# Moving part of the differential attention's weights and of its sub-norm from VectorE to ScalarE and GpSimd

## The chip, the cores and the metric

The kernel runs on one core of a Trainium2 chip. The metric is the device time of one execution in microseconds (us). The engines are called as in the profile: PE (TensorE, matrix products; PEld is its weight load), DVE (VectorE), ACT (ScalarE), POOL (GpSimd) and SP (SyncE, which issues most DMAs). Each engine works through its own queue in order.

## The reference

One layer of a diffusion backbone: 512 latent tokens and 256 context tokens, width 2048, float32. A modulated RMSNorm feeds two mixers: differential attention (8 heads) and latent attention (8 heads); both go through one output projection into the residual stream, and a gated MLP with a short convolution follows. What matters here, cut:

```python
def _diff_attend(q, k, v, lam):
    ...
    w = jax.nn.softmax(s1, axis=-1) - lam * jax.nn.softmax(s2, axis=-1)
    return jnp.einsum('bhqk,bhkd->bhqd', w.astype(v.dtype), v)
...
def _merge_heads(o_da, o_mla, subln_w, lambda_init):
    o_da = _rmsnorm(o_da, subln_w) * (1.0 - lambda_init)
    ...
    return jnp.concatenate([o_da, o_mla], axis=-1)
```

So each differential head makes two softmax maps, subtracts the second times lambda from the first, and multiplies by the values; each head's output is then normed over its 128 features (the sub-norm) and scaled.

## The kernel before, in words

Nearly every product is computed in three passes, from a rounded high part and a rest of each operand (`split`, L77; `mm3`, L101). ACT rounds (L80, L83), DVE subtracts (L81, L84). The layer runs in stages: norm and modulation, input projection, differential attention, latent attention, output projection, MLP. In the stages touched by the change the program is written head by head, and the framework's scheduler decides the order of the instructions on each engine; in the first stage and from the end of the output projection on, the order on PE, ACT, DVE and SP is written out by hand.

**Differential attention** (`da_head`, L551). A head has 4 blocks of 128 queries. For each block `scores_softmax` (L506) is called twice, once per map: four matmuls into a PSUM tile `s` of two buffers (L510), the negated row maximum on DVE (L512), the exponential on ACT with its row sum (L514). DVE takes the reciprocal of both sums (L566). POOL scales the second map by its reciprocal and by minus lambda (L567). Then L568, the changed line, scales the first map and adds the second in one DVE instruction, in place. The tile of the first map, `p0`, has 8 buffers (two heads), that of the second 3. When the four blocks are there, `weighted_values` (L517) goes over the 6 blocks of 128 keys: four transposes on PE into `pt`, which has one buffer (L522), rounding on ACT (L80, `wth`), rest on DVE (L81, `wtl`), and three matmuls with the values into `po` (L104 to L106). ACT copies the output (L525) and SP stores it to DRAM (`o_d`, L572). Between these, PE works on the query projection of the coming heads (`feature`, L457; the matmuls `f<-a2k`); after the last head's projection there is no more of this work.

**Latent attention** (L657 to L674) has the same shape with one map per head. DVE normalises the map (L667, L668). Per pair of heads `latent_pair` (L591) makes queries, keys and values. Between the maps and the weighted values of each head stands `sub_norm(h)` (L646) for the differential head of the same number: load `o_d`, square on ACT (L651), sum over the partitions with a matmul against ones (L653), then `rstd` (L157) and the application (L655).

`rstd` computes the inverse root by a logarithm and an exponential on ACT (L159, L160) and refines it by one Newton step on DVE (L161 to L164). Its tiles `sq` (the square, then the mean), `sr` and `s2` have one buffer each, so the next head's sub-norm writes them again. `rstd` is also called elsewhere (L310, L438, L1301).

**After it**, each of the 16 head outputs is split (L696: ACT L80, DVE L81 to `a2k`), and the output projection (L735) goes over them in the order of the heads, differential ones first. There POOL adds squares for the next norm (L705: one add of 128x512, two inputs from SBUF) and stores the residual (L751), while DVE also computes the modulation (L171).

Of the kernel before, what the change touches and what calls it, by code (L numbers as in the profile page):

```python
# [9 lines left out]
F32 = mybir.dt.float32  # L10
F32R = mybir.dt.float32r
BF16 = mybir.dt.bfloat16
AF = mybir.ActivationFunctionType
ALU = mybir.AluOpType
# [3 lines left out]
P = 128  # L18
D = 2048
KT = D // P  # L20
T = 512
# [31 lines left out]
def layer_kernel(ctx: ExitStack, tc: tile.TileContext, small, rope, c_row, cc_row, x_t, ctx_t, ada, ada_k,  # L53
                 w_g0, w_f, w_v, w_uqn, w_uqr, w_ukv, w_o, w_up0, w_up, w_dn, out_t):
    nc = tc.nc
    pe, ve, sc, gp = nc.tensor, nc.vector, nc.scalar, nc.gpsimd
# [8 lines left out]
    def nm(s):  # L65
        n[0] += 1
        return f"{s}{n[0]}"

    def s_tile():
        return ps_s.tile([P, 1024], F32, tag="s", name=nm("s"))  # L70
# [3 lines left out]
    def b_tile(tag="b", bufs=None):  # L74
        return ps_b.tile([P, 512], F32, tag=tag, name=nm(tag), bufs=bufs or nb[0])
# [44 lines left out]
    def col(name, j=0):  # L120
        o = OFF[name] + j
        return smt[:, o:o + 1]
# [5 lines left out]
    epst = cst.tile([P, 1], F32, name="epst")  # L128
# [7 lines left out]
    subs = cst.tile([P, 1], F32, name="subs")  # L136
# [20 lines left out]
    def rstd(out, ssq, dim, t1, t2):  # L157

        sc.activation(out, ssq, AF.Ln, bias=epst, scale=1.0 / dim)  # L159
        sc.activation(out, out, AF.Exp, scale=-0.5)  # L160
        ve.tensor_scalar(out=t1, in0=ssq, scalar1=1.0 / dim, scalar2=EPS, op0=ALU.mult, op1=ALU.add)  # L161
        ve.scalar_tensor_tensor(out=t2, in0=out, scalar=-0.5, in1=out, op0=ALU.mult, op1=ALU.mult)
        ve.tensor_tensor(t2, t2, t1, op=ALU.mult)
        ve.scalar_tensor_tensor(out=out, in0=t2, scalar=1.5, in1=out, op0=ALU.add, op1=ALU.mult)  # L164
# [101 lines left out]
    with tc.manual_schedule(engines={mybir.EngineType.PE, mybir.EngineType.Activation, mybir.EngineType.DVE,  # L266
# [23 lines left out]
        for kt in range(KT):  # L290
            sq = st.tile([P, TT], F32, tag="h", name=nm("sq"), bufs=3) if kt else sqs
# [39 lines left out]
    for i in range(2):  # L331
        o = OFF["lam"] + 128 * i
        ve.tensor_tensor_reduce(out=lt, in0=smt[:, o:o + 64], in1=smt[:, o + 64:o + 128], op0=ALU.mult,
                                op1=ALU.add, scale=1.0, scalar=0.0, accum_out=ls[:, i:i + 1])
# [9 lines left out]
    for kt in range(KT):  # L344
# [8 lines left out]
        with tc.high_priority():  # L353
            h = st.tile([P, TT], F32, tag="h", name=nm("h"), bufs=3)
            for i, (x, c, m, (hh, hl)) in enumerate(((xs[kt], slice(0, T), modx, hx[kt]),
# [3 lines left out]
                                        op0=ALU.mult, op1=ALU.mult)  # L359
# [123 lines left out]
    for half in range(2):  # L483
        s0, s1, b0, b1_ = s_tile(), s_tile(), b_tile(), b_tile()
# [21 lines left out]
    def scores_softmax(mms, pool, tag, bufs, l):  # L506
        s = s_tile()
        for c0, c1 in ((0, T), (T, TT)):
            for i, (a, b) in enumerate(mms):
                pe.matmul(s[:, c0:c1], a, b[:, c0:c1], start=i == 0, stop=i == len(mms) - 1)  # L510
        m = sm.tile([P, 1], F32, tag="m", name=nm("m"), bufs=4)
        ve.tensor_reduce(out=m, in_=s[:, :TT], axis=AX.X, op=ALU.max, negate=True)  # L512
        p = pool.tile([P, TT], F32, tag=tag, name=nm(tag), bufs=bufs)
        sc.activation(p, s[:, :TT], AF.Exp, bias=m, accum_out=l)  # L514
        return p

    def weighted_values(pool, ws, v, dst, last=False):  # L517
        po = b_tile("po", 1)
        for kt in range(NKEY):
            pt = b_tile("f", 2) if last and kt % 3 else b_tile("pt", 1)  # L520
            for qt in range(NQT):
                pe.transpose(pt[:, qt * P:(qt + 1) * P], ws[qt][:, kt * P:(kt + 1) * P], ident)  # L522
            wth, wtl = split_tiles(pool, ("wth", "wtl"), [P, T], 2, pt)
            mm3(po, v(kt), (wth, wtl), kt == 0, kt == NKEY - 1)
        sc.copy(dst, po)  # L525
# [25 lines left out]
    def da_head(h, qs):  # L551
        ks = da.tile([P, 2, TT], F32R, tag="ks", name=nm("ks"), bufs=2)
        kl = klz[h % 2]
        for i, r in enumerate((lo, hi)):
            nc.sync.dma_start(ks[r].bitcast(F32), k_d[h][0].rearrange("(i p) n -> p i n", i=2))
            nc.sync.dma_start(kl[r, i].bitcast(F32), k_d[h][1][r])
        v = da.tile([P, 2, NKEY, P], F32R, tag="v", name=nm("v"), bufs=2)
        nc.sync.dma_start(v.bitcast(F32), v_d[h // 4][h % 4])
        ws = []
        for qt in range(NQT):  # L560
            c = slice(qt * P, (qt + 1) * P)
            l = sm.tile([P, 2], F32, tag="l", name=nm("l"), bufs=4)
            ps = [scores_softmax([(qs[i][:, c], ks[:, i]), (qs[i][:, c], kl[:, i])], da, f"p{i}", (8, 3)[i],
                                 l[:, i:i + 1]) for i in range(2)]
            rl = sm.tile([P, 2], F32, tag="rl", name=nm("rl"), bufs=4)
            ve.reciprocal(rl, l)  # L566
            gp.tensor_scalar(out=ps[1], in0=ps[1], scalar1=rl[:, 1:2], scalar2=neglam, op0=ALU.mult, op1=ALU.mult)  # L567
            ve.scalar_tensor_tensor(out=ps[0], in0=ps[0], scalar=rl[:, 0:1], in1=ps[1], op0=ALU.mult, op1=ALU.add)  # L568
            ws.append(ps[0])
        o = da.tile([P, T], F32, tag="o", name=nm("o"), bufs=2)  # L570
        weighted_values(da, ws, lambda kt: (v[:, 0, kt], v[:, 1, kt]), o)
        nc.sync.dma_start(o_d[h], o)  # L572

    for h in range(NH):
        da_head(h, da_queries(h))
# [54 lines left out]
    mb = None  # L630
# [4 lines left out]
    def b2k(dt=F32):  # L635
        return bp.tile([P, 512], dt, tag="b2k", name=nm("b2k"))

    oraw = [None] * 16
    mb = tc.alloc_tile_pool(name="mb", bufs=1, side="right", reuse_waits="tile")
# [6 lines left out]
    def sub_norm(h):  # L646

        q, rs, t2 = (mb.tile([P, T], F32, tag=g, name=nm(g), bufs=1) for g in ("sq", "sr", "s2"))
        oraw[h] = b2k()
        nc.sync.dma_start(oraw[h], o_d[h])  # L650
        sc.square(q, oraw[h])  # L651
        po = b_tile("f", 2)
        pe.matmul(po, ones32, q, start=True, stop=True)  # L653
        rstd(rs, po, P, mb.tile([P, T], F32, tag="sq", name=nm("s1"), bufs=1), t2)
        ve.scalar_tensor_tensor(out=oraw[h], in0=oraw[h], scalar=subs, in1=rs, op0=ALU.mult, op1=ALU.mult)  # L655

    for h in range(NH):  # L657
        i = h % 2
        if i == 0:
            qs, qn, kn, vs = nxt  # L660
        ws = []
        for qt in range(NQT):
            c = slice(qt * P, (qt + 1) * P)
            l = sm.tile([P, 1], F32, tag="ml", name=nm("ml"), bufs=4)
            p = scores_softmax([(qn[i][0][:, c], kn[i][0]), (qn[i][0][:, c], kn[i][1]), (qn[i][1][:, c], kn[i][0]),
                                (qs[i][:, c], krh), (qs[i][:, c], krlz[:, i])], mb, "w", 8, l)
            ve.reciprocal(l, l)  # L667
            ve.tensor_scalar(out=p, in0=p, scalar1=l, scalar2=None, op0=ALU.mult)  # L668
            ws.append(p)
        if i == 0 and h + 2 < NH:  # L670
            nxt = latent_pair(h // 2 + 1)
        sub_norm(h)
        oraw[8 + h] = b2k()
        weighted_values(mb, ws, lambda kt: [v[:, i * P:(i + 1) * P] for v in vs[kt]], oraw[8 + h], h == NH - 1)  # L674
# [33 lines left out]
    for dt in range(KT):  # L708
        ve.scalar_tensor_tensor(out=a2[:, dt:dt + 1], in0=modx[:, 64 + dt:65 + dt], scalar=1.0,
                                in1=col("n2", dt), op0=ALU.add, op1=ALU.mult)  # L710
# [24 lines left out]
    for g in range(3):  # L735
        if g % 2:
            outs = [b_tile() for _ in range(4)]
        else:
            s0, s1 = s_tile(), s_tile()
# [74 lines left out]
    hf, hx, t1, t2, t3, t4 = ([None] * KT for _ in range(6))  # L814
# [599 lines left out]
```

## Time and profile before

| | |
|---|---|
| runs of the kernel | median 2437.37 us (2435.56 to 2440.68, three runs) |
| profiled execution, from its first to its last instruction | 2439.6 us; a time of its own beside that span is not listed |
| mean granted TensorE clock | 0.992 |
| differential attention, some 490 to 680 us | 190 us |
| latent attention with the sub-norms, some 680 to 885 us | 205 us |

The profile is read so: a row of the grouped view has the line of the kernel, engine, operation, output and inputs by their names, shape and count, then busy time in us and the mean of one in ns, then the idle time of the engine just before these instructions with what ended it. A row of the waits has who waited, for whom, and the total in us, the number of waits and the longest. A row of the timeline has start and duration in us. PE overlaps its matmuls, so the duration of one is longer than its distance to the next.

### The profile page before, as it was taken

To read this page: it belongs to the slowest core of one execution; us is meant where nothing else is said; L and a number is where in the kernel's file an instruction comes from. 1 tells how busy PE (TensorE), PEld (TensorE's weight loads), DVE (VectorE), ACT (ScalarE), POOL (GpSimd) and SP (SyncE) were. 2 spreads that over 40 slices of the span, in tenths; PEclk is the share of its full clock that TensorE was granted. 3 is DMA by queue.
4 is the path that set the end of the run, shared out by engine and by line. 5 is a ranking of instruction groups with operands and counts; after the bars stand their busy time and mean duration, and the time that the engine had idled before them with its cause. 6 is when DMAs were issued, how large, how long until landed. Compare 5 with 4: busy or idle time off the path is not lost.

```text
span 2439.6 us, 32889 instructions
## 1 busy us (share of the span) xinstructions
PE 2367.0 (97%) x12758; PEld 1978.4 (81%) x12758; DVE 1735.5 (71%) x2316; ACT 1117.0 (46%) x1696; POOL 220.2 (9%) x244
## 2 busy tenths in 40 slices
PE   6999999999999999999999999999999999999998
PEld 3678877777777778889888888888888888888888
DVE  6668876388868878378667676767666666666667
ACT  4432121155646542245445454545454545454545
POOL 0000000121100003100111111111111111111110
PEclk9999999999999999999999999999999999999999
DMA  8758889555411149423555555555555565556573
GB/s 300 279 211 309 327 319 330 181 166 144 127 59 44 44 161 349 146 87 113 147 130 143 134 140 137 137 139 136 141 134 143 132 143 132 141 135 140 133 188 111
DMA packets 130707, 403.32 MB, mean 165 GB/s; under 512 B 14323, under 2 KB 25075, under 8 KB 122099
## 3 DMA queue, kind: packets, MB, share of 16 engines
q1 hardware_dynamic: 104118, 350.87, 43.7%
q0 software_dynamic: 25280, 49.30, 11.6%
q8 instruction: 100, 1.64, 0.3%
q10 hardware_dynamic: 1152, 1.05, 0.1%
q14 instruction: 57, 0.47, 0.1%
HBM read 331.68 MB, written 69.48 MB: 164 GB/s over the span
## 4 chain that ended last, share of the span: by engine, by line
PE 76%; DVE 8%; issue 7%; ACT 4%; DMA 3%; POOL 2%; SPq 0%; DVEq 0%; ACTq 0%; POOLq 0%
PE y L1133 11%; PE b L105 9%; PE b L104 9%; PE b L106 9%; PE z L1133 5%; PE y L1135 5%; PE s L104 3%; PE s L105 3%; PE s L106 3%; PE z L1135 3%; PE s L510 3%; PE x L1133 2%; DMA ada<-in_ada 2%; PE b L206 1%; PE f L104 1%
## 5 line engine op out<-in xcount | busy, mean ns | idle before, releaser
L989 DVE TENSOR_TENSOR wl<-wr,wh 128x1024 fp32r<-128x1024 f32 x144 | 176.4, 1225 | 157.8 <-ACT wh L981 157.1
L981 ACT CAST wh<-wr 128x1024 fp32r<-128x1024 f32 x144 | 151.0, 1049 | 234.0 <-PE b L105 118.5
L104 PE MATMUL b<-ah,wh 128*128 128x512 f32 (+1 forms) x664 | 256.8, 387 | 0.0
L105 PE MATMUL b<-al,wh 128*128 128x512 f32 (+1 forms) x664 | 256.7, 387 | 0.0
L106 PE MATMUL b<-ah,wl 128*128 128x512 f32 (+1 forms) x664 | 255.9, 385 | 0.0
L1154 POOL DMA_DIRECT2D x_d<-xs x160 | 139.6, 1004 | 1162.6 <-ACT xs L1153 1159.3
L989 DVE TENSOR_TENSOR wl<-rb,wh 128x1024 fp32r<-128x1024 f32 x123 | 150.0, 1220 | 126.9 <-ACT wh L981 126.8
L981 ACT CAST wh<-rb 128x1024 fp32r<-128x1024 f32 x123 | 129.2, 1050 | 185.7 <-PE b L105 116.1
L989 DVE TENSOR_TENSOR wl<-ws,wh 128x1024 fp32r<-128x1024 f32 x123 | 150.1, 1220 | 90.1 <-ACT wh L981 90.1
L80 ACT CAST wh<-wr 128x1024 fp32r<-128x1024 f32 (+3 forms) x102 | 99.2, 972 | 217.0 <-PE b L106 62.1
L171 DVE CUSTOM_DVE_ANT_0 ada<-ada,cb,smt 128x2048 f32<-128x2048 f32 x64 | 152.5, 2382 | 54.6 <-DMA ada<-in_ada 54.2
L981 ACT CAST wh<-ws 128x1024 fp32r<-128x1024 f32 x123 | 128.2, 1043 | 130.3 <-DVE ws L943 44.3
L1133 PE MATMUL y<-a2k,wh 128*128 128x512 f32 x656 | 164.0, 392 | 0.0
L81 DVE TENSOR_TENSOR wl<-wr,wh 128x1024 fp32r<-128x1024 f32 (+3 forms) x102 | 116.9, 1146 | 62.1 <-ACT wh L80 61.7
L104 PE MATMUL b<-a2k,wh 128*128 128x512 f32 (+1 forms) x376 | 141.6, 377 | 5.9 <-ACT a2k L838 4.3
L106 PEld LDWEIGHTS b<-ah,wl 128*128 128x128 f32 x664 | 124.8, 188 | 25.7
L104 PEld LDWEIGHTS b<-ah,wh 128*128 128x128 f32 x664 | 125.1, 188 | 22.9
L105 PEld LDWEIGHTS b<-al,wh 128*128 128x128 f32 x664 | 125.1, 188 | 21.9
L105 PE MATMUL b<-a2k,wh 128*128 128x512 f32 (+1 forms) x376 | 140.8, 374 | 0.0
L106 PE MATMUL b<-a2k,wl 128*128 128x512 f32 (+1 forms) x376 | 140.0, 372 | 0.0
L1133 PEld LDWEIGHTS y<-a2k,wh 128*128 128x128 f32 x656 | 118.6, 189 | 21.6
L1133 PE MATMUL y<-b2k,wh 128*128 128x512 f32 x410 | 107.8, 393 | 0.0
(454 smaller groups left out, 5757.2 us busy)
## 6 DMA issues: line engine op xcount, KB each, us to landing
ada<-in_ada SPq DMA_DIRECT2D x64, 1024.0 KB, 6.4
rb<-in_w_up SPq DMA_DIRECT2D x123, 512.0 KB, 4.3
wr<-in_w_dn SPq DMA_DIRECT2D x88, 512.0 KB, 4.3
x_d<-xs POOLq DMA_DIRECT2D x160, 256.0 KB, 6.0
wr<-in_w_up SPq DMA_DIRECT2D x53, 512.0 KB, 4.2
wr<-in_w_f SPq DMA_DIRECT2D x34, 512.0 KB, 6.0
ada<-in_ada SPq DMA_DIRECT2D x32, 512.0 KB, 6.4
adak<-in_ada_k SPq DMA_DIRECT2D x32, 512.0 KB, 6.3
```

The source lines that it names most:

```text
L80: sc.copy(dst_h, src)
L81: ve.tensor_tensor(dst_l, src, dst_h.bitcast(F32), op=ALU.subtract)
L104: pe.matmul(out, st[0], mv[0], start=start, stop=False, **kw)
L105: pe.matmul(out, st[0], mv[1], start=False, stop=False, **kw)
L106: pe.matmul(out, st[1], mv[0], start=False, stop=stop, **kw)
L171: ve.tensor_tensor_reduce(out=junk, in0=w, in1=vec, op0=ALU.mult, op1=ALU.add, scale=1.0, scalar=col("b_ada", j), accum_out=dst[:, j:j + 1])
L510: pe.matmul(s[:, c0:c1], a, b[:, c0:c1], start=i == 0, stop=i == len(mms) - 1)
L981: sc.copy(t, raw[:, k * n_:k * n_ + n_])
L989: ve.tensor_tensor(t, raw[:, k * n_:k * n_ + n_], hi[k].bitcast(F32), op=ALU.subtract)
L1133: pe.matmul(o, w[j][0], hs[j], start=start and j == 0, stop=False, skip_group_check=True)
L1135: pe.matmul(o[:, h0], w[j][1], hs[j][:, h0], start=False, stop=j == 7, skip_group_check=True)
L1154: gp.dma_start(x1_d[dt], x, accum_op=ALU.add)
```

## The change

The second half of each differential weight, `p0 * rl0 + p1`, is done in two instructions in place of one: ACT scales the first map by its reciprocal, POOL adds the second map. In the sub-norm, `rstd` is no longer called. ACT makes the logarithm and the exponential as before, and besides the mean (a second read of the PSUM sum, `Identity`) and the head's output times its weight. POOL makes the Newton step in four instructions and the last product. DVE does nothing there any more. `rstd` itself and its other callers stay as they are.

```diff
@@ da_head
             gp.tensor_scalar(out=ps[1], in0=ps[1], scalar1=rl[:, 1:2], scalar2=neglam, op0=ALU.mult, op1=ALU.mult)
-            ve.scalar_tensor_tensor(out=ps[0], in0=ps[0], scalar=rl[:, 0:1], in1=ps[1], op0=ALU.mult, op1=ALU.add)
+            sc.mul(ps[0], ps[0], rl[:, 0:1])
+            gp.tensor_tensor(out=ps[0], in0=ps[0], in1=ps[1], op=ALU.add)
@@ sub_norm
-        rstd(rs, po, P, mb.tile([P, T], F32, tag="sq", name=nm("s1"), bufs=1), t2)
-        ve.scalar_tensor_tensor(out=oraw[h], in0=oraw[h], scalar=subs, in1=rs, op0=ALU.mult, op1=ALU.mult)
+        s1 = mb.tile([P, T], F32, tag="sq", name=nm("s1"), bufs=1)
+        sc.activation(rs, po, AF.Ln, bias=epst, scale=1.0 / P)
+        sc.activation(s1, po, AF.Identity, bias=epst, scale=1.0 / P)
+        sc.activation(rs, rs, AF.Exp, scale=-0.5)
+        sc.mul(oraw[h], oraw[h], subs)
+        gp.tensor_tensor(out=t2, in0=rs, in1=rs, op=ALU.mult)
+        gp.tensor_tensor(out=t2, in0=t2, in1=s1, op=ALU.mult)
+        gp.tensor_scalar(out=t2, in0=t2, scalar1=-0.5, scalar2=1.5, op0=ALU.mult, op1=ALU.add)
+        gp.tensor_tensor(out=rs, in0=rs, in1=t2, op=ALU.mult)
+        gp.tensor_tensor(out=oraw[h], in0=oraw[h], in1=rs, op=ALU.mult)
```

Counted over the program, DVE issues 72 instructions fewer, ACT 48 more and POOL 72 more; PE issues the same matmuls in another order, since the scheduler orders the two attention stages anew.

## The prediction, made before the result was known

> **What bounds the kernel now.** I read the page first, then the busy time by stretches, then the waits of the stretch that the change touches.
>
> ```profile
> span 2439.6 us, 32889 instructions
> PE 2367.0 (97%) x12758; PEld 1978.4 (81%) x12758; DVE 1735.5 (71%) x2316; ACT 1117.0 (46%) x1696; POOL 220.2 (9%) x244
> ```
>
> TensorE (PE) is busy 97% of the span, so what it loses has to be sought stage by stage. The columns of the next view are the stretch, its length, then PE, weight loads, DVE, ACT and POOL with their counts.
>
> ```profile
> 490.00:650.00 160.00, 156.78 (x772) 122.54 (x772) 139.42 (x202) 93.94 (x176) 34.01 (x30) 0.99 0.50 147
> 650.00:680.00 30.00, 23.49 (x112) 17.18 (x111) 28.25 (x43) 17.68 (x35) 5.62 (x5) 0.97 0.26 95
> 680.00:885.00 205.00, 196.02 (x1061) 156.38 (x1061) 157.98 (x275) 114.46 (x222) 1.47 (x2) 1.00 0.15 48
> 885.00:1040.00 155.00, 155.00 (x685) 128.34 (x685) 88.96 (x81) 42.04 (x49) 26.08 (x23) 1.00 0.71 254
> 490.00:680.00 190.00, 180.28 (x882) 139.72 (x883) 167.67 (x244) 111.62 (x211) 39.63 (x35) 0.99 0.46 138
> ```
>
> Differential attention fills 490 to 680, latent attention with the sub-norms 680 to 885. PE idles 3.2 us up to 650, 6.5 in 650 to 680 (no feature product is left there to fill waits, and DVE is busy 28.25 of 30), 9.0 in latent attention, and nothing from 885 to 1040. So the output projection gives back no delay and offers no gain: whatever the change wins or loses before 885 moves the end by as much, and all that can be won is these 18.7 us.
>
> ```profile
> PE pt L522 <- DVE p L568: 5.4, 7, 2.1
> PE s L510 <- ACT p L514: 2.0, 3, 0.8
> PE po L105 <- DVE wtl L81: 1.1, 3, 0.6
> ```
>
> In 490 to 680 the largest wait of PE is for the finished weights p, which the changed line makes: 5.4 us in 7 waits. How they are made shows in the rows of one pair of maps:
>
> ```profile
> 586.08 0.36 PE L510 MATMUL s<-klz,qs 128*128 128x256 f32 x1
> 586.48 0.96 DVE L512 TENSOR_REDUCE m<-s 128x1 f32<-128x768 f32 x1 [0.61 <-PE s L510]
> 587.53 0.90 ACT L514 ACTIVATE p<-s,m 128x768 f32<-128x768 f32 x1 [0.16 <-DVE m L512]
> 588.33 0.96 DVE L512 TENSOR_REDUCE m<-s 128x1 f32<-128x768 f32 x1 [0.23 <-PE s L510]
> 588.33 0.19 ACT L514 ACTIVATION_READ_ACCUMULATOR p<-s,m 128x1 f32 x1
> 589.20 0.16 DVE L566 RECIPROCAL rl<-l 128x2 f32<-128x2 f32 x1
> 589.46 0.98 POOL L567 TENSOR_SCALAR p<-p,rl,neglam 128x768 f32<-128x768 f32 x1 [11.40 <-DVE rl L566]
> 590.47 1.02 DVE L568 SCALAR_TENSOR_TENSOR p<-p,rl,p 128x768 f32<-128x768 f32 x1 [1.12 <-POOL p L567]
> ```
>
> Scores end at 586.44, the weights at 591.49: 5.05 us, of which 0.7 is the reciprocal standing behind the next pair's reduction on DVE. Free of queues the chain takes 4.35 us.
>
> **The differential maps: work moved.** The rows of the parts:
>
> ```profile
> L568 DVE SCALAR_TENSOR_TENSOR p<-p,rl,p 128x768 f32<-128x768 f32 x32 | 32.5, 1015 | 9.5 <-POOL p L567 9.0
> L567 POOL TENSOR_SCALAR p<-p,rl,neglam 128x768 f32<-128x768 f32 x32 | 37.5, 1173 | 146.3 <-DVE rl L566 141.3 <-ACT p L514 5.1
> L80 ACT CAST wh<-wr 128x768 fp32r<-128x768 f32 x1 | 0.8, 841 | 1.0 <-PE f L105 1.0
> L705 POOL TENSOR_TENSOR ss<-ss,sq x11: 1285/1729/2769, 919.3 to 1011.5; 128x512 f32<-128x512 f32 x11
> ```
>
> DVE loses 32 x 1.015 = 32.5 of its 167.67 us. ACT gains 32 scalings; the nearest row of that width from SBUF to SBUF is the 841 ns cast, so 27 us, to 139 of 190. POOL gains 32 adds with two inputs. No such add of 768 columns is in the trace; the nearest is L705 at 512: times 768/512 it is 1.93 us at its fastest, 2.6 at its median, 4.2 at its slowest. I take 2.0, near the fastest, because L705's slow ones fall beside DVE's modulation products, which this stage lacks; the ends stay for the range. The 32 adds make 64 us, POOL 104 of 190: no bound by its sum.
>
> The chain, however, changes. POOL's multiply and ACT's scaling now run side by side (0.98 against 0.84), then the add follows: 4.35 - 1.02 + 2.0 = 5.3 us, about 1 us longer. Where an exponential of the next pair (0.90 + 0.19) stands between on ACT's in-order queue, it is 6.3.
>
> **What covers that chain.** In the instruction order of both built kernels I counted the matmuls between a pair's last scores and its first transpose. Their pitch:
>
> ```profile
> 586.51 0.40 PE L106 MATMUL f<-a2k,wl 128*128 128x512 f32 x1
> 586.75 0.39 PE L104 MATMUL f<-a2k,wh 128*128 128x512 f32 x1
> 588.82 0.59 PEld L522 LDWEIGHTS pt<-ident,p 128*128 128x128 f32 x4
> ```
>
> That is 0.23 us for 512 columns, half for 256, and 0.147 for a transpose. Cover of the last pair of heads 0 to 7 before: 5.0, 8.0, 7.7, 5.3, 5.5, 6.9, 5.3, 2.7 us. After: 4.8, 10.6, 10.6, 5.1, 4.9, 4.9, 2.9, 3.2. Against 4.35 only head 7 was short, by 1.7; the other 3.7 of the measured 5.4 is queueing. Against the new chain: head 0 is short by 1.4 (an exponential stands ahead of its scaling), head 3 by 0.2, head 4 by 1.2 and head 5 by 1.1 (the output copy L525 stands ahead), head 6 by 2.4, head 7 by 2.1: 8.4 us. Queueing on DVE should fall from 3.7 to about 3, as DVE goes from 88% to some 75% busy (its 135 us plus some 8 of collisions, below). So the transposes wait 11.4 instead of 5.4: **+6 us**. Of the other 4.3 us that PE idles here, waits on DVE's halves (wtl) and on DVE's maxima shrink, while casts on ACT stand behind scalings that wait for a reciprocal; I take **-1.5**.
>
> POOL and DVE get in each other's way. The rows beside each other:
>
> ```profile
> 921.98 1.21 DVE L81 TENSOR_TENSOR wl<-wr,wh 128x1024 fp32r<-128x1024 f32 x1
> 924.87 2.77 POOL L705 TENSOR_TENSOR ss<-ss,sq 128x512 f32<-128x512 f32 x1
> 926.42 2.30 DVE L81 TENSOR_TENSOR wl<-wr,wh 128x1024 fp32r<-128x1024 f32 x1
> ```
>
> The same subtraction takes 1.21 us alone and 2.30 where it follows onto POOL's add, which is stretched too. Some 43 DVE operations of this stage read two SBUF tensors; with adds on POOL a third of the time, 14 collide at 0.6 to 1.1 us, 8 to 15 us of DVE time; I put it in the 75% above. The Trainium skill, GPSIMD Engine Reference, section 1 (Specifications), says the same: POOL shares its SBUF interfaces with VectorE and contends with DVE instructions of two SBUF inputs; these rows agree with it. Its section 4.1 (Engine selection) speaks against this change: elementwise work belongs on VectorE, GPSIMD being about twice as slow with two inputs. From its 4497 ns for 2048 columns an add of 768 is 1.7 us by estimate; six heads would then wait 0.3 us less each, and the sum would come to 2439.6.
>
> **The sub-norm.**
>
> ```profile
> L655 DVE SCALAR_TENSOR_TENSOR b2k<-b2k,subs,sr 128x512 f32<-128x512 f32 x8 | 5.9, 743 | 0.0
> L161 DVE TENSOR_SCALAR s<-f 128x512 f32<-128x512 f32 x8 | 5.5, 688 | 2.0 <-ACT sr L159 1.8
> L164 DVE SCALAR_TENSOR_TENSOR sr<-s,sr 128x512 f32<-128x512 f32 x8 | 5.5, 683 | 0.0
> L160 ACT ACTIVATE sr<-sr 128x512 f32<-128x512 f32 x8 | 5.1, 638 | 0.1
> L668 DVE TENSOR_SCALAR w<-w,ml 128x768 f32<-128x768 f32 x32 | 19.6, 617 | 0.4
> ```
>
> DVE sheds five operations per head (L161 to L164 alike), 8 x 3.48 = 28 of 158 us. ACT gains two of 0.64, 10 us, to 125 of 205. POOL, idle there, gains four products of two inputs, 1.29 each at L705's fastest, and one scaling of 0.65 (the 0.98 of L567 times 512/768): 5.8 us per head, 46 in all. What waits behind: the next head's logarithm on ACT overwrites rs only after POOL's last product; 7 to 11 ACT operations stand between, 5 to 8 us, so at most 1 us in one place. Head 7's result comes 3 us later; between its sum and the first projection product that reads it stand 18.8 us of matmuls, so nothing, and 3 us if that cover were gone. L668 may collide with POOL. PE's 9 us here are mostly ACT chains, so I take **-0.5**. DMAs: the same ones are issued; some on SP change places by one or two, and the residual stores on POOL come after its last sub-norm product: nothing.
>
> Sum: +6 - 1.5 - 0.5 = +4, or 2443.6 us against the profiled 2439.6 (its span; no time around it is listed apart). The runs' median, 2437.37, lies 2.2 below that span, so I forecast **2441.4 us**.
>
> **Rivals.** *DVE was the bound* (faster): it is busy 28.25 of 30 us in 650 to 680, and five fewer L568 there take off up to 5; a third of the 9 idle us of latent attention and of the 3.2 before 650 make 4 more. Against it: head 6 lost cover, 5.3 to 2.9. It gives -4 to -12, likeliest -7: 2430.4.
>
> *POOL falls behind* (slower): pairs of a head come every 3.4 to 4.1 us of matmuls. From an add of 2.6 us on, its 1.17 plus 2.6 exceeds 3.7, a backlog builds over four pairs, and the transposes of six heads without cover wait some 2 us more each: +12, 2449.4; it decides from 2.6 us per add. For it: L705's median, scaled, is 2.6. Against it: half of the pairs' spacing is free of two-input DVE work.
>
> *Nothing happens*: feature products hide both chains, as they do at 98% PE busy up to 650; 2437, within 1.
>
> **How the numbers follow.** Forecast (+1 to +7) 0.45, faster rival 0.22, slower rival 0.25, nothing 0.08. About 0.2% (4.9 us) is what a measurement of this kernel can tell from no change. Of the forecast two thirds lie within it, of the faster rival 0.04 in all: faster 0.18, within 0.42, slower 0.40. The range cuts the outer ends of both rivals: 2428 to 2452. The forecast's own range is 2438 to 2444.5.
>
> **What would show it.** Right: POOL's add at 1.9 to 2.4 us; transposes waiting about 11 us for POOL in 490 to 680, most in the last two heads; DVE under 80% there; latent attention 205 us long within 1 or 2; still nothing lost after 885. Wrong: the stretch from the last feature product to latent attention shorter than before (the first rival), adds above 2.6 us and POOL without idle time inside a head (the second), or ACT, held by a scaling that waits for its reciprocal, named ahead of the casts.

## The result, and the profile after

The changed kernel takes 2458.60 us (median of 4 runs, 2453.11 to 2464.52) against 2439.02 for the kernel before in the same measurement: ratio 1.0073, 95% interval 1.0059 to 1.0088. It is slower by about 18 us, where +2 to +4 was forecast and 2452 was the upper end of the range.

The first lines of the page of the changed kernel, then its busy time by stretches (columns as in the prediction):

```profile
span 2462.7 us, 33015 instructions
PE 2371.9 (96%) x12758; PEld 1982.5 (81%) x12758; DVE 1699.6 (69%) x2244; ACT 1151.3 (47%) x1744; POOL 328.5 (13%) x316
```

```profile
490.00:690.00 200.00, 181.93 (x886) 142.64 (x886) 144.94 (x211) 138.47 (x244) 99.65 (x71) 0.96 0.46 139
690.00:900.00 210.00, 194.20 (x1040) 152.91 (x1039) 143.35 (x234) 121.73 (x235) 47.54 (x40) 0.99 0.14 43
910.00:1058.00 148.00, 148.00 (x654) 122.45 (x653) 85.51 (x73) 37.80 (x43) 27.72 (x23) 1.00 0.72 256
```

DVE has shed 36 us and no stretch is shorter for it. PE idles 18 of 200 us in differential attention (3.4 of them before its first score) and 16 of 210 in latent attention; from 910 on, in the output projection, it loses nothing. So all of the loss lies in the two attention stages. I measure them by their ends: the first differential score and the last latent value product, in before (first two rows) and after (last two).

```profile
488.95 0.76 PE L510 MATMUL s<-ks,qs 128*128 128x512 f32 x1 [4.60 <-DMA ks<-k_d]
...
885.06 0.39 PE L106 MATMUL po<-wth,mvl 128*128 128x512 f32 x1
```

```profile
493.40 0.77 PE L510 MATMUL s<-ks,qs 128*128 128x512 f32 x1 [4.93 <-DMA ks<-k_d]
...
909.09 0.39 PE L106 MATMUL po<-wth,mvl 128*128 128x512 f32 x1
```

That is 396.1 us before and 415.7 after: +19.6, as much as the medians differ. I call it the attention length. PE's idle time within it rises from 18.9 to 33.3 us, which is 14.4 of the 19.6. Most of the rest are matmuls at half clock: such stretches fill 22.1 us of the length after and 8.6 before (the last section). Besides, 4 more of the projection's matmuls, 0.9 us, stand ahead of its end after. The start itself is no part of the change: it lay between 484 and 493 us in profiles of kernels in which nothing ahead of it differs. The first latent score (L510, s<-knh,qnh) starts at 672.79 before and at 688.01 after, so differential attention grew by 10.8 us and latent attention by 8.8: two losses of nearly one size, one for each half of the change.

**Differential attention.** What PE waited for from 490 to 700 in the changed kernel (total us, times, longest):

```profile
PE pt L522 <- POOL p L569: 11.1, 11, 2.2
PE s L510 <- DMA ks<-k_d: 4.9, 1, 4.9
PE s L510 <- DVE qs L424: 2.2, 2, 1.1
PE pt L522 <- DMA cn<-cq_d: 2.1, 1, 2.1
PE po L104 <- ACT wth L80: 1.4, 2, 0.7
```

```profile
L569 POOL TENSOR_TENSOR p<-p,p x32: 1803/1845/2627, 503.3 to 690.0; 128x768 f32<-128x768 f32 x32
```

The transposes waited 5.4 us for the finished weights before and wait 11.1 now. The 2.1 named after a DMA belongs to them too, as the last pair of head 6 shows (rows of DVE, ACT, POOL, PE's weight loads and PE in turn):

```profile
659.21 0.17 DVE L566 RECIPROCAL rl<-l 128x2 f32<-128x2 f32 x1 [1.12 <-ACT p L514]
659.41 0.94 ACT L568 ACTIVATE p<-p,rl 128x768 f32<-128x768 f32 x1 [0.23 <-DVE rl L566]
658.25 1.83 POOL L569 TENSOR_TENSOR p<-p,p 128x768 f32<-128x768 f32 x1 [0.83 <-POOL p L567]
660.06 1.00 POOL L567 TENSOR_SCALAR p<-p,rl,neglam 128x768 f32<-128x768 f32 x1
661.13 1.81 POOL L569 TENSOR_TENSOR p<-p,p 128x768 f32<-128x768 f32 x1
663.00 0.18 PEld L522 LDWEIGHTS pt<-ident,p 128*128 128x128 f32 x1 [2.50 <-POOL p L569]
663.00 0.48 PE L522 MATMUL pt<-ident,p 128*128 128x128 f32 x1 [2.07 <-DMA cn<-cq_d]
...
664.74 1.05 PE L104 MATMUL f<-cn,wh 128*128 128x512 f32 x2
665.60 0.63 PE L105 MATMUL po<-wtl,v 128*128 128x512 f32 x1
...
668.15 0.63 PE L104 MATMUL f<-cn,wh 128*128 128x512 f32 x1
```

The add ends at 662.94 and the transposes start at 663.00: it is POOL that they wait for. From the reciprocal's end (659.38) to the weights it is 3.56 us here, 2.13 in the pair of before that the prediction shows (589.36 to 591.49). Part of that is a queue: the multiply could start at 659.4 and stands behind the add of the pair ahead until 660.06.

**Latent attention.** Its end in the changed kernel, rows of ACT, POOL and PE in turn:

```profile
899.63 0.59 ACT L80 CAST wth<-pt 128x512 fp32r<-128x512 f32 x1 [1.12 <-PE po L106]
903.48 1.14 ACT L80 CAST a2k<-b2k 128x512 fp32r<-128x512 f32 x2 [3.26 <-POOL b2k L664]
904.52 0.58 ACT L80 CAST wth<-f 128x512 fp32r<-128x512 f32 x1
897.62 1.04 POOL L660 TENSOR_TENSOR s<-sr 128x512 f32<-128x512 f32 x1 [12.60 <-ACT sr L658]
...
902.18 1.26 POOL L664 TENSOR_TENSOR b2k<-b2k,sr 128x512 f32<-128x512 f32 x1
905.15 0.80 PE L104 MATMUL po<-wth,mvh 128*128 128x512 f32 x1 [2.87 <-ACT wth L80]
```

POOL works on head 7's sub-norm, five operations, from 897.62 to 903.44. ACT's next instruction splits that result for the projection and waits 3.26 us for it. Behind it in ACT's in-order queue stands the cast of the transposed weights of the last head (wth), whose operands were long ready, and PE waits 2.87 us for that cast. The products behind the wait follow each other every 0.43 us instead of 0.23 until 908, which costs another 1.4 us.

### The profile page after: what moved, and what is told of

The parts are those of the page before. It is cut to its first block, busy times and chain, and to the rows that moved or that the text cites. A ratio compares the mean times of both kernels' runs of the same rounds, so it can differ in the third digit from the quotient of the medians.

```text
span 2462.7 us, 33015 instructions
## 1 busy us (share of the span) xinstructions
PE 2371.9 (96%) x12758; PEld 1982.5 (81%) x12758; DVE 1699.6 (69%) x2244; ACT 1151.3 (47%) x1744; POOL 328.5 (13%) x316
## 4 chain that ended last, share of the span: by engine, by line
PE 84%; DVE 6%; ACT 4%; DMA 3%; issue 2%; POOL 1%; SPq 0%; DVEq 0%; ACTq 0%; POOLq 0%
PE y L1142 12%; PE b L105 10%; PE b L104 10%; PE b L106 10%; PE z L1142 6%; PE y L1144 6%; PE z L1144 3%; PE s L104 3%; PE s L106 3%; PE s L105 3%; PE s L510 3%; PE x L1142 2%; DMA ada<-in_ada 2%; PE f L104 1%; PE f L105 1%
## 5 line engine op out<-in xcount | busy, mean ns | idle before, releaser
L81 DVE TENSOR_TENSOR wl<-wr,wh 128x1024 fp32r<-128x1024 f32 (+3 forms) x102 | 122.5, 1203 | 61.7 <-ACT wh L80 57.9
L512 DVE TENSOR_REDUCE m<-s 128x1 f32<-128x768 f32 x96 | 91.1, 953 | 34.4 <-PE s L510 34.0
```

Source lines behind the costliest of these rows:

```text
L81: ve.tensor_tensor(dst_l, src, dst_h.bitcast(F32), op=ALU.subtract)
```

## The experiments

Each kernel is compared with runs of the kernel before on the same chip. "Excess" is the time by which matmuls of a kind start later than the work ahead of them accounts for, summed from their rows. All ratios have the 95% interval beside them; the attention length is that of the profiled run (396.1 before, 415.7 after).

### Each half alone

The differential maps of the change, with the old sub-norm:

> Only the differential maps are changed (scaling on ACT, add on POOL); the sub-norm is as before. Theory A, the add on POOL makes the weights late: the transposes wait for POOL some 15 us in place of 6, and the time is 8 to 11 us above before, about half of the change's +19. Theory B, the sub-norm is the whole cost: within 3 us of before. Theory C, any new order of the scheduler costs: some +5 to +10, but with waits that do not name POOL's add.

Measured 2452.90 us, 1.0047 [1.0030, 1.0064], length 407.5. The stage before latent attention is as long as in the whole change (193.7 us; whole change 194.6), and the transposes' excess is 15.0 us (6.4 before).

The sub-norm of the change, with the old maps:

> Only the sub-norm is changed; the maps are as before. Theory A: differential attention as long as before, latent attention 8 to 10 us longer, of which some 4 us is one wait near its end (ACT's split of head 7 waiting for POOL's last product, with casts of latent head 7 queued behind it). Theory B: +17 to +20. Theory D, POOL idle in latent attention hides the sub-norm: within 2 us of before.

Measured 2449.61 us, 1.0033 [1.0022, 1.0043], length 405.5. Here differential attention is as before (184.6 us, 183.8 before) and latent attention 8.6 us longer. The halves add up: 11.5 and 8.1 us make 19.6, the whole 17.8 with an interval of some 3.6 to either side. Neither half hides or feeds the other.

### The maps: which of the two moved operations costs

Scaling on ACT, add on DVE (e3); scaling on DVE, add on POOL (e4):

```diff
-            ve.scalar_tensor_tensor(out=ps[0], in0=ps[0], scalar=rl[:, 0:1], in1=ps[1], op0=ALU.mult, op1=ALU.add)
+            sc.mul(ps[0], ps[0], rl[:, 0:1])                                     # e3
+            ve.tensor_tensor(ps[0], ps[0], ps[1], op=ALU.add)                    # e3
+            ve.tensor_scalar(out=ps[0], in0=ps[0], scalar1=rl[:, 0:1], scalar2=None, op0=ALU.mult)   # e4
+            gp.tensor_tensor(out=ps[0], in0=ps[0], in1=ps[1], op=ALU.add)        # e4
```

> The first map is scaled on ACT, but the second is added on DVE; sub-norm as before. If POOL's add is what costs (theory A): within 3 us of before, as the chain is 4.3 us again and DVE keeps its 1 us per pair. If ACT's queue is what costs, with a scaling that waits for the reciprocal standing ahead of casts and exponentials (theory E): +6 to +10, like the maps alone.

> The first map is scaled on DVE in an instruction of its own (as L668 does, 0.62 us), the second is added on POOL; sub-norm as before. Theory A: +8 to +11, transposes waiting for POOL as in the maps alone. Theory E: within 3 us of before, since ACT has no new work.

e3: 2436.56 us, 0.9982 [0.9972, 0.9991], length 390.8: faster than before. e4: 2452.65 us, 1.0044 [1.0029, 1.0059], length 409.8. So the scaling on ACT costs nothing, and POOL's add is the whole loss. PE's waits for the weights in e3 and in e4, 490 to 700:

```profile
PE pt L522 <- DVE p L569: 1.1, 2, 0.9
```

```profile
PE pt L522 <- POOL p L569: 14.2, 13, 1.9
```

In e3 the wait of 5.4 us is down to 1.1. Two things could do that: the scaling no longer waits for POOL's multiply, or the scheduler, which orders the stage anew for every kernel, put more matmuls ahead of the transposes. The traces part them. From the end of the reciprocal to the finished weights a pair takes 2.48 us in before, 3.09 in e3 and 3.59 in the change. These are means of all 32 pairs; I call them the mean chain. So behind the reciprocal e3's chain is no shorter than that of before, and it is the order of the instructions that took the wait away: heads 0, 3, 4 and 5 have more cover, and in head 6, which has less, the reciprocal comes 1.5 us sooner after the last scores (3.0 instead of 4.5). The cover of the last pair of heads 0 to 7, in us, counted in the built kernels as in the prediction (before and after stand there):

| kernel | head 0 | 1 | 2 | 3 | 4 | 5 | 6 | 7 |
|---|---|---|---|---|---|---|---|---|
| e1, as the whole change | 4.8 | 10.6 | 10.6 | 5.1 | 4.9 | 4.9 | 2.9 | 3.2 |
| e3 | 7.5 | 9.4 | 8.5 | 9.2 | 8.0 | 7.5 | 3.2 | 3.2 |
| e4 | 5.3 | 9.5 | 8.8 | 5.0 | 5.0 | 4.2 | 3.7 | 1.7 |
| e7 (below) | 5.2 | 8.5 | 5.9 | 5.0 | 5.3 | 4.7 | 4.4 | 2.9 |
| e13 (below) | 8.2 | 12.4 | 8.5 | 10.0 | 6.8 | 7.6 | 5.0 | 3.3 |
| e14 (below) | 7.5 | 9.4 | 8.5 | 9.2 | 8.0 | 7.5 | 6.6 | 3.2 |

With the add on POOL (e1, e4) heads 0, 3, 4 and 5 have 4.2 to 5.3 us of cover, with the add on DVE (e3) 7.5 to 9.2. So part of the 16 us between e1 and e3 is the order that comes with the add's engine, on top of a chain that is 0.5 us longer.

Half of the add's columns on POOL, half on DVE:

```diff
+            sc.mul(ps[0], ps[0], rl[:, 0:1])
+            gp.tensor_tensor(out=ps[0][:, :384], in0=ps[0][:, :384], in1=ps[1][:, :384], op=ALU.add)
+            ve.tensor_tensor(ps[0][:, 384:], ps[0][:, 384:], ps[1][:, 384:], op=ALU.add)
```

> Maps: scaling on ACT, columns 0 to 383 added on POOL and 384 to 767 on DVE at the same time, so that the chain has half of POOL's add (some 0.95 us in place of 1.85); sub-norm as before. Theory, length of the chain: transposes wait 6 to 8 us, the time is within 4 us of before. Rival, what costs is that POOL and DVE share their way to SBUF: both halves block each other, and it stays at +8 or more.

Measured 2446.62 us, 1.0019 [1.0006, 1.0031], length 402.3, transposes' excess 10.4. Two groups of its trace, 490 to 690 (busy us, mean ns | idle before):

```profile
L569 POOL TENSOR_TENSOR p<-p,p 128x384 f32<-128x384 f32 x32 | 38.0, 1188 | 11.2 <-POOL p L567 5.9 <-issue 2.6 <-ACT p L568 1.3
L570 DVE TENSOR_TENSOR p<-p,p 128x384 f32<-128x384 f32 x32 | 28.2, 882 | 4.2 <-POOL p L567 2.6 <-ACT p L568 1.6
```

Side by side neither half is half as long: POOL's 384 columns take 1.19 us, and DVE's take 0.88, nearly the 0.95 of a whole add in e3. The mean chain is 3.28 us instead of 3.59, the cover is no better than e1's but in head 6 (1.5 us more), and the transposes wait less; the loss falls with it.

### The maps: the later weights, or the contention

POOL's add does two things: it ends the chain of a pair later, and it stretches DVE's operations of two SBUF tensors. These are rows of the changed kernel, DVE first, then POOL:

```profile
531.57 3.60 DVE L424 SCALAR_TENSOR_TENSOR qs<-rt,qs 64x512 fp32r<-64x512 f32 x2
530.44 1.95 POOL L567 TENSOR_SCALAR p<-p,rl,neglam 128x768 f32<-128x768 f32 x1
532.47 2.14 POOL L569 TENSOR_TENSOR p<-p,p 128x768 f32<-128x768 f32 x1
```

The two products took 0.69 us each in before and 1.8 here, and POOL's multiply 1.95 instead of 0.98. To part the two, first the wait was covered: the next head's maps are emitted ahead of this head's values, so that from head 1 on some 12 us or more of matmuls stand between the last scores and the transposes (7.8 in head 7 of e10). Alone (e10), with POOL's add (e11), and with the add on DVE (e15):

```diff
     for h in range(NH):
-        da_head(h, da_queries(h))
+        maps = da_head(h, da_queries(h))    # ends after the maps
+        if head:
+            da_values(*head)                # weighted_values and the store of the head before
+        head = maps
+    da_values(*head)
```

> Arithmetic and engines as before, but each differential head's weighted values are issued after the next head's maps, so that the matmuls between a pair's last scores and its first transpose grow from 3 to 8 us to 12 to 16 us for all heads but the first. Theory, the length of the chain against that cover is what PE loses: waits of the transposes go from 6.4 to about 1 to 2 us, 3 to 6 us faster than before. If DVE's load is the limit of this stage: no change within 2 us.

> The same later values, with the change's maps (scaling on ACT, add on POOL); sub-norm as before. Theory of the cover: POOL's add costs nothing once 12 us or more cover it, so the time is within 2 us of the kernel with later values alone, and 10 us or more below the maps alone. Rival, POOL and DVE hinder each other: still 5 us or more above later values alone.

> The maps of the next head are emitted ahead of the values of this one, ScalarE scales, VectorE adds: the run with the later values and GpSimd's add (1.0047) with only the add's engine changed, both with 12 us or more of matmuls ahead of the first transposes. If covered weights leave only collisions and the stage's late start, this is 0.999 to 1.002 and 6 us below that run. If the late start alone explains that run, it is 1.003 to 1.005.

e10: 2444.47 us, 1.0013 [1.0003, 1.0024], length 390.4. e11: 2452.81 us, 1.0047 [1.0028, 1.0066], length 400.5. e15: 2447.96 us, 1.0040 [1.0027, 1.0053], length 393.9. The cover works on what it was made for: in e11 the transposes' excess is 3.1 us instead of 15.0. The time doesn't come back, so my theory that late weights were the whole cost of the maps fell in this form. Two things took their place. The new order has a price at its start: the attention stage begins at 495 us in all three, after a wait of some 11 us (4.6 before). And with POOL's add other waits grow; PE from 490 to 700 in e10, then in e11:

```profile
PE po L105 <- DVE wtl L81: 1.4, 2, 1.0
...
PE pt L522 <- DVE p L568: 0.5, 1, 0.5
```

```profile
PE po L105 <- DVE wtl L81: 4.6, 5, 1.4
PE pt L522 <- POOL p L569: 2.7, 3, 1.4
```

The low halves that DVE makes of the transposed weights now come late. Between e15 and e11, which differ in the add's engine alone, the length differs by 6.6 us, the ratios by less than their intervals; how the covered cost divides is not settled by these. Nor is the scaling on ACT free in this order: e15 is 3.5 us longer than e10, and PE waits 2.9 us for ACT's casts (wth) in it instead of 1.2.

So each suspect was then made alone, on e3 as the base. e13 puts a pass over the finished weights on POOL into the chain, with one input tensor; e14 puts a POOL add of two tensors beside the chain, into a scratch tile that nothing reads:

```diff
             sc.mul(ps[0], ps[0], rl[:, 0:1])
             ve.tensor_tensor(ps[0], ps[0], ps[1], op=ALU.add)
+            gp.tensor_scalar(out=ps[0], in0=ps[0], scalar1=1.0, scalar2=None, op0=ALU.mult)     # e13
+            gp.tensor_tensor(out=jk, in0=ps[0], in1=ropet.rearrange("p a t -> p (a t)")[:, :TT], op=ALU.add)   # e14
```

> Maps: ScalarE scales, VectorE adds (as in the run whose ratio was 0.998), and then GpSimd multiplies the finished weights by 1.0 in place, one operation of one input tensor (about 1.0 us) per pair, so the chain is as long as with the add on GpSimd, or a little longer, while GpSimd reads one tensor instead of two; sub-norm as before. Late weights theory: the latency is the cost, so 1.003 to 1.006, with the transposes waiting 12 us or more on GpSimd. Collision theory: two-input adds on GpSimd beside VectorE are the cost, so 0.998 to 1.000.

> Maps: ScalarE scales, VectorE adds, and GpSimd then makes one more 768-column add of two tensors per pair into a scratch tile that nothing reads, so GpSimd works as long as in the changed kernel and beside the same stage, but outside the chain; sub-norm as before. Collision theory: 1.002 to 1.005, VectorE's two-tensor operations stretched by 8 us or more in sum. Late weights theory: 0.998 to 1.000, VectorE stretched but nothing on TensorE late.

e13: 2463.02 us, 1.0093 [1.0075, 1.0110], length 419.4. The pass took twice what I had expected, and POOL's multiply of the next pair often stands behind it, so that DVE's adds wait 16.3 us for the multiply (2.2 in e3). The mean chain is 5.89 us, 2.8 longer than e3's, not 1:

```profile
L569 DVE TENSOR_TENSOR p<-p,p 128x768 f32<-128x768 f32 x30 | 28.6, 955 | 17.1 <-POOL p L567 16.3 <-ACT p L568 0.6
L570 POOL TENSOR_SCALAR p<-p x32: 2128/2132/3035, 497.1 to 698.6; 128x768 f32<-128x768 f32 x32
```

```profile
PE pt L522 <- POOL p L570: 17.6, 13, 2.7
...
PE s L510 <- DVE qs L424: 0.8, 2, 0.5
```

DVE's products for the queries (qs) keep a mean of 0.70 us in it. So a longer chain costs by itself, with hardly any stretching: 27 us above e3, its base, for 2.8 us per pair, although the table gives it about as much cover as e3 (only head 4 has less, by 1.2 us). e14: 2458.04 us, 1.0073 [1.0057, 1.0089], length 412.3. The largest of its waits within the stage, 490 to 700, and the groups of DVE's query products and adds:

```profile
PE s L510 <- DVE qs L424: 6.0, 7, 1.3
PE po L105 <- DVE wtl L81: 5.9, 9, 1.3
PE pt L522 <- DVE p L570: 5.0, 6, 2.1
```

```profile
L424 DVE SCALAR_TENSOR_TENSOR qs<-rt,qs 64x512 fp32r<-64x512 f32 x14 | 18.4, 1316 | 0.4
L570 DVE TENSOR_TENSOR p<-p,p 128x768 f32<-128x768 f32 x30 | 28.7, 957 | 10.5 <-POOL p L568 8.9 <-ACT qs L423 0.9 <-ACT p L514 0.3
```

Only 5.0 us fall to the transposes (5.4 in before, 1.1 in e3), and they wait for DVE. The order of its matmuls is nearly e3's (the table), and the kernel stands 22 us above e3, as far as the whole change does, much of it through operands that DVE makes late: qs and wtl make 11.9 us of waits (1.4 in e3), and the query products take a mean of 1.32 us instead of 0.69. But the scratch add isn't as far from the chain as I had meant it to be. It waits for DVE's add, and POOL's next multiply stands behind it. DVE's adds wait 8.9 us for that multiply (2.2 in e3), and with them all that follows in DVE's queue, and the mean chain is 3.54 us, as long as the change's. In e13 DVE stood still longer (16.3 us) without making qs late (0.8 us), so the stretching is the likelier cause of the late queries; that all of the 22 us are contention is not shown. So late weights alone can cost as much as the change (e13), and the contention can reach PE (e14), at a price that stays open. The expectations, of which each let only one be expensive, were too narrow.

In the change itself the waits say which one bears more: 13.2 us of the transposes for POOL (7.8 more than before), 2.2 for qs, 0.5 for wtl. There the late weights are the greater part and the contention the smaller; with cover (e11) it is the other way round. The exact share is not settled, since one add makes both and brings an order of its own.

### The sub-norm: which part costs

ACT's part as in the change, POOL's five operations done by DVE (four, two of them fused):

```diff
         sc.activation(rs, po, AF.Ln, bias=epst, scale=1.0 / P)
         sc.activation(s1, po, AF.Identity, bias=epst, scale=1.0 / P)
         sc.activation(rs, rs, AF.Exp, scale=-0.5)
         sc.mul(oraw[h], oraw[h], subs)
+        ve.scalar_tensor_tensor(out=t2, in0=rs, scalar=-0.5, in1=rs, op0=ALU.mult, op1=ALU.mult)
+        ve.tensor_tensor(t2, t2, s1, op=ALU.mult)
+        ve.scalar_tensor_tensor(out=rs, in0=t2, scalar=1.5, in1=rs, op0=ALU.add, op1=ALU.mult)
+        ve.tensor_tensor(oraw[h], oraw[h], rs, op=ALU.mult)
```

> Sub-norm with the change's four ScalarE instructions, but with the refinement and the last product on DVE; maps as before. If POOL's slow chain is what the sub-norm costs: within 3 us of before, and ACT waits for no one at the splits of the heads. If the two further ACT instructions per head are what costs (casts come later): most of the +8 us stays.

Measured 2441.74 us, 1.0001 [0.9992, 1.0010], length 400.2. The length misleads here: 18 more of the projection's matmuls than in before stand ahead of the last value product, 4.1 us at 0.23 us each, and without them it is that of before. ACT's extra operations cost nothing; POOL's chain is the loss.

The change's sub-norm for heads 0 to 6, the old one for head 7:

```diff
+        if h == NH - 1:
+            rstd(rs, po, P, mb.tile([P, T], F32, tag="sq", name=nm("s1"), bufs=1), t2)
+            ve.scalar_tensor_tensor(out=oraw[h], in0=oraw[h], scalar=subs, in1=rs, op0=ALU.mult, op1=ALU.mult)
+            return
```

> The change's sub-norm for heads 0 to 6, the old one for head 7; maps as before. Theory: the wait of ACT on POOL's last product of head 7 (3.3 us, with clock lost behind it) is half of the sub-norm's cost, so +3 to +5 in place of +8. If POOL's collisions with DVE and its buffers all through the stage are the cost: still +7 or more.

Measured 2443.16 us, 1.0006 [0.9996, 1.0015], length 398.4. In this order seven heads on POOL cost 1 us or so; the eighth, the only one behind which PE's last casts stand, costs the other 6 to 7. So the place decides, not the sum of POOL's work.

Then head 7 was moved out of that place: its sub-norm emitted right behind head 6's (e9), or every head's emitted one head earlier (e16):

```diff
-        sub_norm(h)
+        if h < NH - 1:          # e9
+            sub_norm(h)
+        if h == NH - 2:
+            sub_norm(NH - 1)
+        if h + 1 < NH:          # e16, with sub_norm(0) ahead of the loop
+            sub_norm(h + 1)
```

> The change's sub-norm for all heads, but head 7's is issued together with head 6's, before head 7's maps; maps as before. Theory, the cost of the sub-norm is ACT standing at head 7's split with casts queued behind it: that wait goes, and the time is within 2 us of before, in place of +8. If POOL's collisions all through the stage are the cost: +5 or more stays.

> Sub-norm on ScalarE and GpSimd as in the change, but every head's sub-norm is emitted one head earlier (head 0 ahead of the first latent head), so none stands ahead of the last casts and no two stand together; maps as before. If the in-order wait of ScalarE's split behind GpSimd's last product, and the crowding of three sub-norms, were the whole cost: 0.999 to 1.001. If GpSimd's chain also costs in the middle of the stage (late tiles, collisions with VectorE): 1.002 to 1.004.

e9: 2447.66 us, 1.0032 [1.0023, 1.0042], length 403.8. e16: 2450.67 us, 1.0042 [1.0028, 1.0056], length 406.6. Both miss: moved away from the end, the sub-norms on POOL cost as much as before. The tail's wait is gone or smaller, and others come. ACT's waits in e9 (690 to 910) and in e16 (690 to 915):

```profile
ACT sr L655 <- POOL b2k L663: 4.8, 3, 2.2
...
ACT a2k L80 <- POOL b2k L663: 1.7, 1, 1.7
```

```profile
ACT sq L651 <- DMA krlz<-kr_d: 4.6, 1, 4.6
ACT sr L655 <- POOL b2k L663: 4.1, 3, 1.9
...
ACT sq L651 <- POOL s L660: 2.8, 2, 1.7
```

The tiles sq, sr and s2 have one buffer each. The next sub-norm's square and logarithm on ACT overwrite them, and wait until POOL is through; the casts that PE needs stand behind. In e16 the first square waits for a load as well. Whether this is the whole of what is left there was not tried. So the 1 us of e6 belongs to its order of instructions; it is not the price of seven sub-norms on POOL wherever they stand.

### Repairs together, and a better version

The whole change with both repairs, the later values and head 7's early sub-norm:

> The whole change, with both covers: values issued later, head 7's sub-norm issued early. Theory: about 20 us below the change, 3 to 6 us faster than before. Rival (load on POOL and its collisions): at most half of the +19 us goes.

Measured 2458.67 us, 1.0073 [1.0055, 1.0090], length 407.1: no better than the change. The attention is 8.6 us shorter than in the change's profile, but it starts at 495 us, after the same wait of some 11 us, where kernels with the old order start between 484 and 493.

ACT's share of both halves, all of POOL's returned to DVE (e3 and e5 together):

> Scaling of the maps on ACT with the add on DVE, and the sub-norm's further instructions on ACT with its refinement on DVE: the change without any new work on POOL. If POOL is all that costs: 3 to 7 us faster than before. If ACT's load begins to tell in latent attention: no faster than before.

Measured 2438.35 us, 0.9984 [0.9973, 0.9994], length 396.8 (392.7 without the 18 projection matmuls that stand ahead of its end as in e5). It and e3 (0.9982) beat the kernel before, by some 4 us; all that they gain is in e3's one line.

## Why the prediction was wrong

**What bounds the kernel** held: PE loses time where an operand is late and in the matmuls at half clock that follow, nothing is given back after attention, and PE is at 148.00 of 148 us from 910 on.

**The chain of the maps: right in mechanism, mis-sized.** POOL's add was taken at 2.0 us and took 1.85; by the estimate from the Trainium skill, GPSIMD Engine Reference, section 3.1 (its 4497 ns for 2048 columns), it would have been 1.7, and the trace lies between. The transposes were to wait 11.4 us and waited 13.2. The chain itself became 1.1 us longer on average (2.48 to 3.59), as forecast ("about 1 us longer"). The term "+6" should have been 7.8 by the waits and 8.8 by their excess (6.4 to 15.2), and the half as a whole cost 11.5 (e1). Counting the cover head by head was right: by it, heads 0 and 3 to 7 were to be short, these six wait and heads 1 and 2 do not, and e3, with 2.5 to 4 us more in four of them, hardly waits. Counting it for the last pair alone was not. Of the 13.2 us only 5.3 fall to the last pair's transposes, for which 8.4 were forecast; 6.6 fall to the third pair's (0.2 in before) and 1.3 to head 0's first. A wait for the third pair gives the last one time, so in heads 0, 4, 5 and 6 the two together come out near the forecast (1.3, 1.2, 1.2 and 2.8 us against 1.4, 1.2, 1.1 and 2.4), but in heads 3 and 7 they are 0.9 and 2.2 us above it (1.1 and 4.3). That 11.4 comes as near to 13.2 as it does is in part luck. What the term left out is what follows a wait: PE's clock falls after it (below), and queries and halves come late where POOL's add meets DVE. The contention itself I had put at 8 to 15 us of DVE time and in DVE's share alone, never on PE's path; by e14 it can reach PE through qs and wtl.

**"-1.5" for the other waits failed.** Waits on wtl (1.1 to 0.5) and on ACT's exponentials, which follow DVE's maxima (2.0 to nothing), shrank as said, but qs (2.2) and wth (1.4) took their place: up to the last differential value product, all matmuls but the transposes start 16.9 us later than the work ahead of them accounts for in before, and 16.6 in after.

**"-0.5" for latent attention failed, and with it the sign of that half: it costs +8.** The step was "Head 7's result comes 3 us later; between its sum and the first projection product that reads it stand 18.8 us of matmuls, so nothing". I counted cover for PE's product that reads the result. The first reader is ACT's split, and behind that, in order, stood casts for which PE had no cover at all. The step beside it, "at most 1 us" for the next head's logarithm, held in the change, where ACT waited 0.9 us, but not in e2 with the same sub-norm (2.9). e6 and e2 together show the place: without head 7, +1; with it, +8. Of that, the rows of the change show PE's wait of 2.87 us and 1.4 us of slow products behind it; the rest is spread over the stage and was not taken apart.

**The rivals.** *DVE was the bound* fell: DVE is at 72% in 490 to 690, as forecast (below 80%), and PE gained nothing by it. *POOL falls behind* gave +12, near to what the maps cost, but for another reason: it was to decide from 2.6 us per add, and the add took 1.85. A milder form of it shows at 660.06, where a multiply stood 0.7 us behind the add of the pair ahead. No rival had ACT's queue in latent attention in it, and the range ended 7 us short.

## What to carry to other kernels

When an operation moves to a slower engine, look past the consumer on the critical engine to the first instruction anywhere that reads the result, and then at what stands behind that reader in its in-order queue: cover has to be counted to there. A unit of work with time around it may run on a slow engine seven times for next to nothing and cost its full price the eighth time, at the end of the stage; moving it ahead is no repair by itself, since other readers stand there (e9, e16). Freeing an engine that is at 88% of a stage is worth nothing when the bound is how late single operands come. And where a scheduler orders the matmuls, count the cover anew for every variant, and of every operand, not only of the last: the same two operations with the add on DVE came with 3 us more of it in four heads.

## What the runs showed of the hardware that was not expected

- **A wait of PE costs more than its length.** From 663.00 on, 512-column products follow each other every 0.43 us instead of 0.23 (665.60 and its neighbours, still so at 668.15). From 664.15 to 668.58 eight such products and four transposes took 4.43 us, and at their usual pitch 8 x 0.23 + 4 x 0.147 = 2.43: another 2.0 us. The granted clock shows why. These are stretches of the changed kernel around this wait and around the one at the end of latent attention (columns as before; the first number behind POOL's is the clock):

```profile
658.80:662.20 3.40, 1.36 (x6) 0.51 (x4) 1.40 (x4) 2.35 (x4) 3.32 (x3) 1.00 0.69 218
662.20:669.10 6.90, 5.43 (x15) 4.16 (x16) 4.72 (x7) 2.12 (x4) 0.74 (x1) 0.51 1.01 372
901.20:904.60 3.40, 1.08 (x7) 0.64 (x5) 0.47 (x1) 1.12 (x3) 2.17 (x2) 1.00 0.50 176
904.60:908.00 3.40, 2.85 (x7) 2.30 (x8) 3.40 (x7) 3.40 (x8) 0.00 (x0) 0.50 0.75 292
```

  The clock is at half from 662.2, only 1.3 us after PE's last product ahead of the wait (it ends at 660.93). It changes on a grid of 3.41 us that the wait doesn't shift, by how busy PE was in the stretch before: 1.36 and 1.08 of 3.4 us here. Over the 18 profiles of this case, 480 to 955 us, 2429 such stretches ran at full clock. All 37 in which PE was busy 45% or less were followed by half clock, 17 of the 44 between 45% and 60%, and none above. The Trainium skill, TensorE: Matmul & The Clock Gate, section "What's actually happening", says that an idle window of about 3.4 us halves the clock until a busy one has passed; the factor and the length agree with these rows, but here the window need not be idle.
- **POOL and DVE slow each other.** Beside POOL's add, DVE's products of two SBUF tensors took 1.8 us instead of 0.69, and POOL's multiply 1.95 instead of 0.98; two half adds side by side took 1.19 us on POOL and 0.88 on DVE (e7).
- **POOL's price depends on the form.** Multiplying 768 columns by a constant in one step took 2.13 us (e13, hardly spread), while the multiply by two column scalars took 0.98 at the same width; a square of one tensor, 512 columns, took 1.04 us, and a product of two tensors 1.28.
